# Expert input biases on two halves of the array's rows: a mixture-of-experts block on one Trainium2 core

## The chip, the cores and the metric

The kernel runs on one core of a Trainium2 chip. A core has a matrix engine (TensorE, in the profile PE, with its weight loads as PEld), a vector engine (VectorE, DVE), a scalar engine (ScalarE, ACT), a general engine (GpSimd, POOL) and a queue engine (SyncE, SP) that issues most transfers. They run side by side and wait for each other by semaphores. The metric is the device time of one execution in microseconds (us); the median over runs counts.

## The reference

The reference computes two transformer blocks on 512 tokens of 1024 numbers. The change touches the first block's mixture of experts: a router picks 4 of 32 experts for each token, and each expert, on its tokens (padded to blocks of 128), computes

```
xb = t_pad[tok_idx]                       # 128 tokens x 1024
hb = xb @ w_exp_in[e] + b_exp_in[e]       # 128 x 2048: gate columns, then value columns
g = jnp.minimum(hb[:, :D_FF], SWIGLU_LIMIT)
u = jnp.clip(hb[:, D_FF:], -SWIGLU_LIMIT, SWIGLU_LIMIT)
a = g * jax.nn.sigmoid(SWIGLU_ALPHA * g) * (u + 1.0)
return a @ w_exp_out[e] + b_exp_out[e]
```

`b_exp_in` is a table of 32 experts by 2048 columns, 1024 of the gate and 1024 of the value. It is the addition of this row that the change rearranges.

## The kernel before

All weights are float32. Each is split into a high part (a copy rounded to the matrix engine's format, by ACT, line 149, `whi`) and a low part (the difference, by DVE, line 151, `wlo`), and each product is made of three matmuls (lines 137, 138, 139: high by high, high by low, low by high). The first stage (`block1`) is a layer norm, the projections, two kinds of attention and an output projection (`out_proj`), with a layer norm and the routing tile by tile at its end. Then come the 32 experts (`moe`), one after the other, and then the second block.

An expert (`moe_h`) has four accumulators of 128 tokens x 512 columns in PSUM: `hb[0]`, `hb[1]` for the gate and `hb[2]`, `hb[3]` for the value. Each is opened with one matmul that adds the bias (line 879), and then takes 8 row blocks of `w_exp_in[e]`, three matmuls each. `swiglu` (line 884 on) makes the activation, and `moe_y` multiplies it by `w_exp_out[e]`. The second product of expert e-1 is computed while expert e is being opened, so that bias matmuls of e stand between matmuls of e-1.

The bias matmul picks a row out of the table. `self.bin` is a tile of 128 partitions x 2048 columns: rows 0 to 31 hold the high part of the 32 experts' biases, rows 32 to 63 the low part, rows 64 to 127 are zero. `self.e64` has column e equal to one in rows e and 32+e and zero elsewhere; broadcast to 128 columns it is the stationary operand, so that every token gets the row of expert e, high plus low. All 128 rows of the array are used, half of them with zeros. `moe_bias` (lines 751 to 762) loads and splits the table while the output projection of the first block runs: four transfers on POOL's queue, two ACT copies, two DVE differences, two ACT copies and a POOL memset of the zero rows.

If an expert has more than 128 tokens, `overflow` (line 963 on) handles the further blocks in a loop whose number of turns is read on the device. It has its own bias column (`ove`) on 64 rows. The inputs here make no turn of it: its tiles appear nowhere in the trace.

The order of instructions on each engine is set by a scheduler when the program is built. It also gives out the buffers: a pool `S` of 17 large buffers, a pool `H` of 10 buffers of up to 1024 numbers per partition, and four PSUM banks `mm`. A transfer into a buffer is issued when its last reader is done, and the SP queue is strictly in order. Loads of expert weights (`raw`, line 198) are issued ahead of use.

Of the kernel before, what the change touches and what calls it, by code (L numbers as in the profile page):

```python
# [11 lines left out]
F32 = mybir.dt.float32  # L12
FR = mybir.dt.float32r
# [3 lines left out]
AF = mybir.ActivationFunctionType  # L17
OP = mybir.AluOpType
AX = mybir.AxisListType
# [45 lines left out]
def f(ap):  # L65
    return ap.bitcast(F32)
# [27 lines left out]
class K:  # L94
# [539 lines left out]
    def moe_consts(self):  # L634
        nc, c, a = self.nc, self.const, self.a
        self.wr = self.slot([128, 8, 32], F32, "wr")
        nc.scalar.dma_start(self.wr, a["w_router"].rearrange("(k p) e -> p k e", p=128))
        self.br = c.tile([128, 32], F32, name="br")
        ap = a["b_router"]
        nc.scalar.dma_start(self.br, bass.AP(tensor=ap.tensor, offset=ap.offset, ap=[[0, 128], [1, 32]]))  # L640

        it = self.w([128, 512], I32, "s")
        nc.gpsimd.iota(it[:, :128], pattern=[[1, 128]], base=1, channel_multiplier=0)
        self.iota1 = c.tile([128, 128], F32, name="iota1")
        nc.vector.tensor_copy(self.iota1, it[:, :128])
        self.iota32 = c.tile([128, 32], F32, name="iota32")
        nc.vector.tensor_scalar(self.iota32, self.iota1[:, :32], -1.0, None, op0=OP.add)
        it = self.w([128, 512], I32, "s")
        nc.gpsimd.iota(it[:, :128], pattern=[[1, 128]], base=0, channel_multiplier=-1)
        self.tri = c.tile([128, 128], BF, name="tri")  # L650
        nc.vector.tensor_scalar(self.tri, it[:, :128], 0.0, None, op0=OP.is_gt)
        self.onesb = c.tile([128, 128], BF, name="onesb")
        nc.vector.memset(self.onesb, 1.0)
        self.pidx = c.tile([128, 1], F32, name="pidx")
        nc.vector.tensor_scalar(self.pidx, it[:, 0:1], -1.0, None, op0=OP.mult)
        self.pbig = c.tile([128, 1], F32, name="pbig")
        nc.vector.tensor_scalar(self.pbig, self.pidx, 4096.0, None, op0=OP.add)
        self.pidx1 = c.tile([128, 1], F32, name="pidx1")
        nc.vector.tensor_scalar(self.pidx1, self.pidx, 1.0, None, op0=OP.add)

        e64 = c.tile([128, 32], FR, name="e64")
        nc.gpsimd.memset(f(e64), 0.0)
        for i in range(2):
            sl = slice(32 * i, 32 * i + 32)
            nc.vector.tensor_copy(e64[sl, :], self.ident[sl, sl])
        self.e64 = e64
        self.selb = c.tile([128, 4, 32], BF, name="selb")
        self.posm = c.tile([128, 4, 32], F32, name="posm")

        self.V = c.tile([128, 4, 32, 6], BF, name="V")  # L670
        for i in range(4):
            nc.vector.memset(self.V[:, i, :, 1], 128.0 * i - 4096.0)
        self.m6 = c.tile([128, 6], F32, name="m6")
        nc.vector.memset(self.m6, 1.0)
        nc.vector.memset(self.m6[:, 3:4], 0.0)
        self.gate_in, self.hx = {}, {}
        self.G = c.tile([128, 4, 32], F32, name="G")
        self.ybuf = self.D.tile([2048, 1024], F32, name="ybuf")
        self.identb = c.tile([128, 128], BF, name="identb")
        nc.vector.tensor_copy(self.identb, self.ident)  # L680
# [69 lines left out]

    def moe_bias(self):
        nc, a = self.nc, self.a
        self.bin = self.slot([128, 2048], FR, "bin")
        nc.gpsimd.memset(f(self.bin[64:128, :]), 0.0)
        for c in range(2):
            sl = slice(1024 * c, 1024 * c + 1024)
            raw = self.slot([64, 1024], F32, "braw")
            for i in range(2):
                nc.gpsimd.dma_start(raw[32 * i:32 * i + 32, :], a["b_exp_in"][:, sl])
            nc.scalar.activation(self.bin[:64, sl], raw, AF.Copy)  # L760
            nc.vector.tensor_tensor(raw[32:64, :], raw[32:64, :], f(self.bin[32:64, sl]), op=OP.subtract)
            nc.scalar.activation(self.bin[32:64, sl], raw[32:64, :], AF.Copy)

    def moe_xg(self):
        xg = self.slot([128, 2, 1024], F32, "xg")
# [108 lines left out]
    def moe_h(self, xT, ones, brow, get, hb=None, beside=None):  # L874

        nc = self.nc
        hb = hb or [self.mm() for _ in range(4)]
        for n in range(4):
            nc.tensor.matmul(hb[n], ones, brow[:, n * 512:(n + 1) * 512], start=True, stop=False)
        k = n = 0  # L880
        while k < 8:
            wh, wl = get()
            for c in range(0, wh.shape[1], 512):
                at = self.mm3(hb[n], (xT[0][:, k, :], xT[1][:, k, :]), (wh[:, c:c + 512], wl[:, c:c + 512]), False, k == 7)
                k, n = k + n // 3, (n + 1) % 4
                if beside and n == 0 and k < 8:
                    with self.tc.issue_after(at.ins):
                        next(beside, 0)
        for _ in beside or ():
            pass  # L890
        return hb
# [74 lines left out]
    def overflow(self, free):  # L966

        nc, a = self.nc, self.a
        n = nc.values_load(self.nxi[0:1, 0:1], min_val=0, max_val=16)
        with self.tc.If(n > 0):  # L970
            with self.tc.For_i(0, n, 1) as j:
                t = self.slot([128, 256], F32, "ovf")
                jf, ef, bf, ecol = (t[:, x:x + 1] for x in range(4))
                cum, le, oe = t[:, 32:64], t[:, 64:96], t[:, 96:128]
# [32 lines left out]
                g = self.gates_at(oh, [V[:, i, :] for i in range(4)])  # L1007
                x = self.moe_gather(free, ix)
                xT = self.t128([x[:, :512], x[:, 512:]])
                nc.vector.tensor_scalar(ecol, self.pidx, 32.0, -32.0, op0=OP.is_ge, op1=OP.mult)  # L1010
                nc.vector.tensor_tensor(ecol, ecol, self.pidx, op=OP.add)
                e64 = self.w([64, 2], FR, "ove", 1)
                nc.vector.tensor_scalar(e64[:, 0:1], ecol[:64, :], ef[:64, :], None, op0=OP.is_equal)

                w1 = a["w_exp_in"][bass.ds(er, 1)].rearrange("o (k p) c -> p (o k) c", p=128)
                w2 = a["w_exp_out"][bass.ds(er, 1)].rearrange("o (k p) c -> p (o k) c", p=128)
# [2 lines left out]
                def get():  # L1019
# [1 line left out]
                    nc.sync.dma_start(raw, next(it))  # L1021
                    self.split(raw, hi, lo)
                    return hi, lo
                hb = self.moe_h(xT, e64[:, 0:1].to_broadcast([64, 128]), self.bin[:64, :], get)
                aT = self.t128(self.swiglu(hb), 0.5)
                self.y_out(self.moe_y(aT, get), ix, g)

# [872 lines left out]
```

## Time and profile before

| | |
|---|---|
| median of three runs | 2116.5 us (2109.83, 2116.5, 2118.72) |
| the profiled execution | 2119.69 us, its span 2117.5 us |
| busy, share of the span | PE 95%, PEld 76%, DVE 77%, ACT 60%, POOL 13% |
| mean granted TensorE clock | 0.965 of full |
| experts opened | from 444.3 to 1592.0 us |
| transfers | 513.25 MB, mean 242 GB/s |

The span is from the first to the last instruction that the profiler saw; the execution is 2.2 us longer. A matmul's row in the trace gives its start, its duration and its form. The form `128*128` is the part of the array in use, rows by columns; `64*128` is a product on 64 rows. A matmul of 512 columns lasts about 0.39 us, but the next one starts 0.23 us after it, since they are pipelined: the distance of the starts is what a matmul costs in a dense stream, not its duration. Rows that follow each other with the same line and form are merged into one, with their count.

### The profile page before, as it was taken

What the parts mean: (1) busy time and instruction counts of PE and PEld (TensorE: products, weight loads), DVE (VectorE), ACT (ScalarE), POOL (GpSimd) and SP (SyncE); (2) the same over time, 40 slices, a digit from 0 to 9 for tenths busy, and PEclk for the clock granted to TensorE, in tenths of its full rate; (3) what the DMA queues carried; (4) which work ended last, traced back from release to release, by engine and by line L of the source; (5) the groups of instructions that cost most, each with busy time, mean ns of one, the idle gap of its engine ahead of it and who ended that gap; (6) DMA issues with size and microseconds to landing.
All of it is one profiled execution on the core that took longest, in us unless ns stands there. A gap on an engine that the chain in (4) does not pass through costs nothing. (4 is left out here: it accounts for less than half of the span.)

```text
span 2117.5 us, 26074 instructions
## 1 busy us (share of the span) xinstructions
PE 2009.2 (95%) x9868; PEld 1600.5 (76%) x9868; DVE 1629.5 (77%) x2075; ACT 1272.9 (60%) x1407; POOL 274.6 (13%) x224
## 2 busy tenths in 40 slices
PE   5999999969999999999999899999999689999997
PEld 5777778847888888888888688888767578777656
DVE  5574454689898989898989789898888868557644
ACT  3554443246777777787868677786665365356540
POOL 3000000041111010101010010101115300110000
PEclk9999999979999999999999999999999799999969
DMA  5241226637999999999999899999987522242101
GB/s 192 68 147 53 70 71 210 266 120 275 348 375 362 365 367 373 356 370 359 369 359 374 308 361 355 362 370 363 375 336 276 201 73 68 67 111 69 52 32 65
DMA packets 161141, 513.25 MB, mean 242 GB/s; under 512 B 17955, under 2 KB 92995, under 8 KB 112113
## 3 DMA queue, kind: packets, MB, share of 16 engines
q1 hardware_dynamic: 139392, 466.80, 60.1%
q0 software_dynamic: 12592, 29.57, 3.9%
q10 hardware_dynamic: 9024, 15.16, 2.1%
q8 instruction: 79, 1.29, 0.2%
q14 instruction: 54, 0.43, 0.1%
HBM read 498.43 MB, written 29.49 MB: 249 GB/s over the span
## 5 line engine op out<-in xcount | busy, mean ns | idle before, releaser
L151 DVE TENSOR_TENSOR wlo<-raw,whi 128x2048 fp32r<-128x2048 f32 (+1 forms) x464 | 980.3, 2144 | 94.1 <-ACT whi L149 56.7
L149 ACT ACTIVATE whi<-raw 128x2048 fp32r<-128x2048 f32 (+1 forms) x468 | 820.8, 1785 | 161.4 <-PE sc L139 52.3
L138 PE MATMUL mm<-wlo,xT 128*128 128x512 f32 x1024 | 406.4, 397 | 1.9 <-DVE wlo L151 1.9
L139 PE MATMUL mm<-whi,xT 128*128 128x512 f32 x1024 | 404.1, 395 | 0.0
L137 PE MATMUL mm<-whi,xT 128*128 128x512 f32 x1024 | 338.0, 399 | 2.8 <-ACT whi L149 2.8
L138 PEld LDWEIGHTS mm<-wlo,xT 128*128 128x128 f32 x1024 | 194.6, 190 | 49.1 <-DVE wlo L151 11.2
L139 PEld LDWEIGHTS mm<-whi,xT 128*128 128x128 f32 x1024 | 194.2, 190 | 39.0
L137 PEld LDWEIGHTS mm<-whi,xT 128*128 128x128 f32 x1024 | 192.2, 190 | 41.4 <-ACT whi L149 3.5
L138 PE MATMUL sc<-wlo,xT 128*128 128x512 f32 x512 | 201.6, 394 | 2.1 <-DVE wlo L151 2.1
L139 PE MATMUL sc<-whi,xT 128*128 128x512 f32 x512 | 201.5, 394 | 0.0
L931 POOL DMA_INDIRECT ybuf<-h,sx x31 | 99.2, 3200 | 758.1 <-DVE wlo L151 551.6
L137 PE MATMUL sc<-whi,xT 128*128 128x512 f32 x512 | 184.9, 393 | 1.5 <-ACT xT L149 1.5
L149 ACT ACTIVATE xT<-tp 128x512 fp32r<-128x512 f32 x128 | 73.4, 595 | 161.3 <-PE tp L868 160.8
L1155 DVE CUSTOM_DVE_ANT_0 s<-sc,bias 128x512 f32<-128x512 f32 (+3 forms) x101 | 47.2, 487 | 91.8 <-PE sc L145 81.0
L138 PEld LDWEIGHTS sc<-wlo,xT 128*128 128x128 f32 x512 | 97.2, 190 | 23.6 <-DVE wlo L151 2.5
L137 PEld LDWEIGHTS sc<-whi,xT 128*128 128x128 f32 x512 | 97.4, 190 | 22.3 <-ACT xT L149 1.9
L139 PEld LDWEIGHTS sc<-whi,xT 128*128 128x128 f32 x512 | 96.9, 190 | 21.2 <-DVE xT L153 0.5
L137 PE MATMUL mm<-hTh,whi 128*128 128x512 f32 x256 | 106.6, 416 | 0.4 <-ACT whi L149 0.4
L139 PE MATMUL mm<-hTh,wlo 128*128 128x512 f32 x256 | 100.6, 393 | 0.6 <-DVE wlo L151 0.6
L138 PE MATMUL mm<-hTl,whi 128*128 128x512 f32 x256 | 100.8, 394 | 0.0
L1159 ACT ACTIVATE p<-s,mn 128x128 f32<-128x128 f32 (+3 forms) x112 | 62.2, 557 | 60.7 <-DVE mn L1155 56.4
L137 PE MATMUL mm<-xTh,whi 128*128 128x512 f32 (+1 forms) x216 | 91.5, 424 | 0.0
(451 smaller groups left out, 3105.0 us busy)
## 6 DMA issues: line engine op xcount, KB each, us to landing
raw<-in_w_exp_in_dram SPq DMA_DIRECT2D x254, 1024.0 KB, 6.9
raw<-in_w_exp_out_dram SPq DMA_DIRECT2D x128, 1024.0 KB, 7.1
raw<-in_w_in_dram SPq DMA_DIRECT2D x58, 512.0 KB, 4.2
raw<-in_w_out_dram SPq DMA_DIRECT2D x8, 1024.0 KB, 6.3
raw<-in_w_in_dram SPq DMA_DIRECT2D x7, 1024.0 KB, 7.2
yp<-ybuf POOLq DMA_DIRECT2D x12, 512.0 KB, 12.5
x<-in_x_dram SPq DMA_DIRECT2D x4, 512.0 KB, 8.3
hd<-h SPq DMA_DIRECT2D x4, 512.0 KB, 2.6
```

The costliest lines, as they stand in the source:

```text
L137: mm(out, lh, rh, start=start, stop=False, **kw)
L138: mm(out, lh, rl, start=False, stop=False, **kw)
L139: return mm(out, ll, rh, start=False, stop=stop, **kw)
L149: h = nc.scalar.activation(hi, src, AF.Copy, scale=scale)
L151: l = (eng or nc.vector).tensor_tensor(lo, src, f(hi), op=OP.subtract)
L931: self.nc.gpsimd.indirect_dma_start(out=self.ybuf[:, :], out_offset=bass.IndirectOffsetOnAxis(ap=ix[:, 1:2], axis=0), in_=y, in_offset=Non ...
L1155: nc.vector.tensor_tensor_reduce(s[:, :kl], sc[:, :kl], bias, op0=OP.add, op1=OP.min, scale=1.0, scalar=3e38, accum_out=mn)
L1159: nc.scalar.activation(p[:, :kl], s[:, :kl], AF.Exp, scale=-1.0, bias=mn, accum_out=sm)
```

## The change

The table of biases is laid out anew. Rows 0 to 31 now hold the high part of the gate's 1024 columns, rows 32 to 63 their low part, rows 64 to 95 the high part of the value's columns and rows 96 to 127 their low part. `self.bin` has 1024 columns instead of 2048, and no zero rows. `e64` has its identity in all four groups of 32 rows. A bias is added by a matmul on 64 rows: the lower half of the rows for the gate, the upper half for the value. The two follow each other in the program, gate and value of the same 512 columns, then the next 512. In the overflow loop the column `ove` gets 128 rows.

```diff
@@ moe_consts
         e64 = c.tile([128, 32], FR, name="e64")
-        nc.gpsimd.memset(f(e64), 0.0)
-        for i in range(2):
+        for i in range(4):
             sl = slice(32 * i, 32 * i + 32)
             nc.vector.tensor_copy(e64[sl, :], self.ident[sl, sl])
@@ moe_bias
-        self.bin = self.slot([128, 2048], FR, "bin")
-        nc.gpsimd.memset(f(self.bin[64:128, :]), 0.0)
-        for c in range(2):
-            sl = slice(1024 * c, 1024 * c + 1024)
-            raw = self.slot([64, 1024], F32, "braw")
-            for i in range(2):
-                nc.gpsimd.dma_start(raw[32 * i:32 * i + 32, :], a["b_exp_in"][:, sl])
-            nc.scalar.activation(self.bin[:64, sl], raw, AF.Copy)
-            nc.vector.tensor_tensor(raw[32:64, :], raw[32:64, :], f(self.bin[32:64, sl]), op=OP.subtract)
-            nc.scalar.activation(self.bin[32:64, sl], raw[32:64, :], AF.Copy)
+        self.bin = self.slot([128, 1024], FR, "bin", "S")
+        raw = self.slot([128, 1024], F32, "braw")
+        for i in range(4):
+            nc.gpsimd.dma_start(raw[32 * i:32 * i + 32, :], a["b_exp_in"][:, i // 2 * 1024:i // 2 * 1024 + 1024])
+        nc.scalar.activation(self.bin, raw, AF.Copy)
+        for i in (1, 3):
+            ps = slice(32 * i, 32 * i + 32)
+            nc.vector.tensor_tensor(raw[ps, :], raw[ps, :], f(self.bin[ps, :]), op=OP.subtract)
+            nc.scalar.activation(self.bin[ps, :], raw[ps, :], AF.Copy)
@@ moe_h
-        for n in range(4):
-            nc.tensor.matmul(hb[n], ones, brow[:, n * 512:(n + 1) * 512], start=True, stop=False)
+        for n in range(2):
+            for x, hp in enumerate((slice(0, 64), slice(64, 128))):
+                nc.tensor.matmul(hb[n + 2 * x], ones[hp, :], brow[hp, n * 512:(n + 1) * 512], start=True, stop=False)
@@ overflow
-                nc.vector.tensor_scalar(ecol, self.pidx, 32.0, -32.0, op0=OP.is_ge, op1=OP.mult)
-                nc.vector.tensor_tensor(ecol, ecol, self.pidx, op=OP.add)
-                e64 = self.w([64, 2], FR, "ove", 1)
-                nc.vector.tensor_scalar(e64[:, 0:1], ecol[:64, :], ef[:64, :], None, op0=OP.is_equal)
+                nc.vector.tensor_tensor(oe, oe, f(self.e64), op=OP.mult)
+                nc.vector.tensor_reduce(out=ecol, in_=oe, axis=AX.X, op=OP.add)
+                e64 = self.w([128, 2], FR, "ove", 1)
+                nc.vector.tensor_copy(e64[:, 0:1], ecol)
...
-                hb = self.moe_h(xT, e64[:, 0:1].to_broadcast([64, 128]), self.bin[:64, :], get)
+                hb = self.moe_h(xT, e64[:, 0:1].to_broadcast([128, 128]), self.bin, get)
```

On PE the places of the bias matmuls stay; which accumulators they open changes. These rows are of expert 3, the first that runs at the even pace of the middle of the kernel. `mm_1046` to `mm_1049` are its accumulators `hb[0]` to `hb[3]` before, `sc_1027` and `sc_1028` the output of expert 2. Before:

```order
L137 MATMUL sc_1028_4665<-whi_1021_4634,xT_994_4492 128x512
L879 MATMUL mm_1046_4758<-bin_735_3293,e64_3269 128x512
L879 MATMUL mm_1047_4759<-bin_735_3293,e64_3269 128x512
L138 MATMUL sc_1027_4664<-wlo_1022_4635,xT_994_4492 128x512
...
L137 MATMUL sc_1028_4665<-whi_1030_4668,xT_994_4492 128x512
L879 MATMUL mm_1048_4760<-bin_735_3293,e64_3269 128x512
L879 MATMUL mm_1049_4761<-bin_735_3293,e64_3269 128x512
L137 MATMUL mm_1046_4758<-whi_1033_4686,xT_1004_4544 128x512
```

The same place of the changed kernel, where `mm_1045` to `mm_1048` are `hb[0]` to `hb[3]`:

```order
L137 MATMUL sc_1027_4663<-whi_1020_4632,xT_993_4490 128x512
L879 MATMUL mm_1045_4756<-bin_735_3294,e64_3269 128x512
L879 MATMUL mm_1047_4758<-bin_735_3294,e64_3269 128x512
L138 MATMUL sc_1026_4662<-wlo_1021_4633,xT_993_4490 128x512
...
L137 MATMUL sc_1027_4663<-whi_1029_4666,xT_993_4490 128x512
L879 MATMUL mm_1046_4757<-bin_735_3294,e64_3269 128x512
L879 MATMUL mm_1048_4759<-bin_735_3294,e64_3269 128x512
L137 MATMUL mm_1045_4756<-whi_1032_4684,xT_1003_4542 128x512
```

In both, the four biases stand as two twos, twelve matmuls of the expert before apart. Before, the first two are `hb[0]` and `hb[1]`; now they are `hb[0]` and `hb[2]`, one on each half of the rows, and so for the second two. Matmuls on all 128 rows stand ahead of each two and behind it. Over the 32 experts both orders have 51 such twos (two each in experts 3 to 19 and 24 to 30, one each in 1, 2 and 31), 5 fours in a row (experts 0 and 20 to 23) and 6 single ones (two each in 1, 2 and 31).

One `H` buffer less is taken by the table, so later takers of that pool come one buffer earlier. This shows on SP's queue at the end of the first block's output projection (`raw` loads of the last quarter of `w_out`, and of the first expert's weights). Before:

```order
L228 DMA gb_742_3312<-in_ln1_b_dram 128x1024
L198 DMA raw_745_3319<-in_w_out_dram 128x4x512
L198 DMA raw_752_3433<-in_w_exp_in_dram 128x2048
L198 DMA raw_753_3435<-in_w_exp_in_dram 128x2048
L198 DMA raw_754_3437<-in_w_exp_in_dram 128x2048
L198 DMA raw_755_3439<-in_w_exp_in_dram 128x2048
L198 DMA raw_756_3441<-in_w_exp_in_dram 128x1024
L198 DMA raw_757_3443<-in_w_exp_in_dram 128x1024
```

After:

```order
L228 DMA gb_741_3310<-in_ln1_b_dram 128x1024
L198 DMA raw_755_3439<-in_w_exp_in_dram 128x1024
L198 DMA raw_756_3441<-in_w_exp_in_dram 128x1024
L198 DMA raw_744_3317<-in_w_out_dram 128x4x512
L198 DMA raw_751_3431<-in_w_exp_in_dram 128x2048
L198 DMA raw_752_3433<-in_w_exp_in_dram 128x2048
L198 DMA raw_753_3435<-in_w_exp_in_dram 128x2048
L198 DMA raw_754_3437<-in_w_exp_in_dram 128x2048
```

Two half-size loads of the first expert have moved ahead of the last quarter of `w_out`.

## Rows read from the trace of the kernel before

**Rows 1.** The page, busy time of each engine (share of the span), instructions.

```profile
PE 2009.2 (95%) x9868; PEld 1600.5 (76%) x9868; DVE 1629.5 (77%) x2075; ACT 1272.9 (60%) x1407; POOL 274.6 (13%) x224
```

**Rows 2.** Stretches: their us, busy of each engine, clock, DMA share, GB/s.

```profile
553.75:1132.12 578.37, 578.37 (x2704) 474.35 (x2702) 529.17 (x403) 440.41 (x354) 73.77 (x32) 1.00 0.96 365
589.65:625.61 35.96, 35.96 (x170) 29.57 (x169) 33.00 (x27) 27.50 (x23) 4.65 (x2) 1.00 0.97 374
```

**Rows 3.** Line 879 in 553 to 1170 and 1200 to 1510, ns min/median/max.

```profile
L879 PE MATMUL mm<-bin,e x68: 397/397/398, 553.7 to 1132.4; 128*128 128x512 f32 x68
...
L879 PE MATMUL mm<-bin,e x36: 388/397/398, 1217.9 to 1503.4; 128*128 128x512 f32 x36
```

**Rows 4.** Timeline of PE in expert 3: start, us, form, count.

```profile
553.75 0.63 PE L879 MATMUL mm<-bin,e 128*128 128x512 f32 x2
554.22 0.39 PE L138 MATMUL sc<-wlo,xT 128*128 128x512 f32 x1
...
556.97 0.63 PE L879 MATMUL mm<-bin,e 128*128 128x512 f32 x2
557.43 0.62 PE L137 MATMUL mm<-whi,xT 128*128 128x512 f32 x2
```

**Rows 5.** Timeline of PE in the attention; last, the first two of the six.

```profile
234.33 0.39 PE L139 MATMUL mm<-hTh,wlo 128*128 128x512 f32 x1
234.65 0.96 PE L145 MATMUL sc<-qk 64*128 64x512 f32 x6
235.54 0.50 PE L137 MATMUL mm<-hTh,whi 128*128 128x512 f32 x1
235.87 0.40 PE L138 MATMUL mm<-hTl,whi 128*128 128x512 f32 x1
...
234.65 0.50 PE L145 MATMUL sc<-qk 64*128 64x512 f32 x2
```

**Rows 6.** Timeline of PE in the second block, one product on 64 rows.

```profile
2004.39 0.39 PE L139 MATMUL mm<-xTh,wlo 128*128 128x512 f32 x1
2004.71 0.49 PE L145 MATMUL sc<-nk,nq 64*128 64x512 f32 x1
2005.13 0.76 PE L1178 MATMUL mm<-aT,vv 128*64 128x128 f32 x9
```

**Rows 7.** Timeline of PE in expert 22, four biases in a row.

```profile
1253.65 1.09 PE L879 MATMUL mm<-bin,e 128*128 128x512 f32 x4
1254.58 0.39 PE L137 MATMUL mm<-whi,xT 128*128 128x512 f32 x1
```

**Rows 8.** Timeline of PE in expert 2, single biases.

```profile
526.78 0.40 PE L879 MATMUL mm<-bin,e 128*128 128x512 f32 x1
...
527.49 0.40 PE L879 MATMUL mm<-bin,e 128*128 128x512 f32 x1
```

**Rows 9.** Timeline of PE, waits next to biases of experts 0, 1, 20.

```profile
449.94 0.90 PE L868 MATMUL tp<-ident,xg 128*128 128x128 f32 x3 [2.75 <-DMA xg<-h1d,sx]
...
471.66 0.50 PE L138 MATMUL sc<-wlo,xT 128*128 128x512 f32 x1 [2.06 <-DVE wlo L151]
...
1180.88 2.07 PE L879 MATMUL mm<-bin,e 128*128 128x512 f32 x4 [9.86 <-DVEq L970]
```

**Rows 10.** Timeline of PE in expert 31.

```profile
1578.70 1.20 PE L879 MATMUL mm<-bin,e 128*128 128x512 f32 x2
1580.10 2.07 PE L798 MATMUL sc<-bout,gT 32*128 32x512 f32 x2 [0.20 <-DVE acc L800]
```

**Rows 11.** Timeline of SP and ACT at the first output projection.

```profile
367.90 0.38 SPq L198 DMA_DIRECT2D raw<-in_w_out_dram  x1
371.98 23.45 SPq L198 DMA_DIRECT2D raw<-in_w_exp_in_dram  x11
...
390.83 1.92 ACT L149 ACTIVATE whi<-raw 128x2048 fp32r<-128x2048 f32 x1 [14.31 <-DMA raw<-in_w_exp_in_dram]
```

**Rows 12.** SP waits in 553 to 1130: us in total, times, longest.

```profile
SPq L198 <- PE sc L139: 187.3, 65, 3.5
```

## Prediction

> **What bounds the kernel now.** I read the page first: PE is busy 95% of the span, far ahead of the next engine, DVE at 77% [rows 1]. A share over the whole kernel is a mean over stages, so the second view is a table of stretches. From 553.75 to 1132.12 us, experts 3 to 19, PE is busy for all 578.37 us, at full granted clock; DVE is busy 529.17 of them, ACT 440.41, and the DMA engines 96% [rows 2]. One expert is 35.96 us, with PE busy for all of it [rows 2]. A PE that is full by the trace may still wait inside matmuls whose ends are modelled, so I looked at the queue that feeds it: SP's weight loads wait for PE to free a buffer (187.3 us in 65 waits for one line alone) [rows 12]. The transfers are held back by PE and not the other way round. What PE gains or loses per expert goes straight into the time.
>
> The third view is line 879, the bias matmuls. In experts 3 to 19 there are 68 of them, in experts 21 to 29 another 36, all of them on 128 by 128 of the array [rows 3]. What one costs is read from distances of starts: the first two of expert 3 hold the engine from 553.75 to 554.22, the second two from 556.97 to 557.43 [rows 4], so 0.465 us for two and 0.93 us for an expert, of 35.96.
>
> **The price of a product on 64 rows.** Does a two on halves of the rows cost one slot instead of two? The kernel has such products already, in the attention (line 145, form 64\*128). Of six of them, all of 512 columns, the first two together end 0.50 us after the start of the first, while one lasts 0.49 [rows 5, 6]: they run side by side, and a two is one slot of 0.23 us.
>
> But the six also show what it costs to get there and back. From the start of the last full product ahead of them, 234.33, to the start of the second full product behind, 235.87, there are 1.54 us [rows 5]. In these lie five slots: a full product, three twos, a full product, 5 x 0.23 = 1.15. The other 0.39 us are the price of leaving the full array and coming back. Where it lies: the first two start 0.32 after the full product (0.09 late), the full product behind them is followed by the next only after 0.33 (0.10 late), and 0.20 are between [rows 5]. A single product of 512 columns shows the middle: 0.32 from the full product to it, and 0.42 from it to the next one in another form [rows 6], which with 0.33 at the end gives 0.09 + 0.19 + 0.10 = 0.38, the same sum.
> The Trainium skill, "TensorEngine Tiling (Array Packing)", Key Properties, says that going to another tiling mode drains TensorE. The trace agrees, with 0.39 us for the way there and back.
>
> **The sum.** A two before is 0.465; after it is 0.23 + 0.39 = 0.62, so 0.155 us more. The order leaves the places as they were, two twos per expert with full products between them.
> - Experts 3 to 19 and 24 to 30 have 48 twos, and experts 1 and 2 one each: 50 x 0.155 = 7.75 us.
> - Experts 21 to 23 have their four in a row, 0.93 us [rows 7]; after it is two slots and one way there and back, 0.46 + 0.39 = 0.85. 3 x -0.08 = -0.2.
> - Expert 20 opens at the lower clock, its four taking 2.07 us [rows 9]. Two of four slots go, two costlier changes come: -0.3, between -0.8 and +0.1.
> - Expert 2 has two single biases [rows 8]. A product on 64 rows takes a full slot, and each pays both ways: 2 x 0.39 = +0.8.
> - Expert 1's two single ones stand ahead of waits of PE, 2.75 us for gathered tokens and 2.06 us for a DVE difference [rows 9], which take up 0.4 each; the first wait covers expert 0's four as well. Cost 0.
> - Expert 31's stand among products of forms that are not full anyway (32\*128) [rows 10], so the changes of form are paid today: -0.1.
>
> Together 7.75 - 0.2 - 0.3 + 0.8 - 0.1 = 7.95, say 8 us.
>
> The trace shows no single two of 512 columns between full products, so I bound the 0.39. From below: if only the middle part is paid, 0.19 [rows 6], a two costs 0.42 and 50 of them save 2.3 us; with two singles at 0.19 and the other places -1, the whole is -3. From above: 0.19 at either end and 0.10 at the last, 0.48, gives 50 x 0.245 = 12.3 and 13 in all. I take 0.39, the row with the same form, length and neighbours.
>
> Beside the bias matmuls, the table is made differently while the output projection runs. ACT has three copies instead of four, DVE the same two differences, POOL loses a memset and keeps four transfers. ACT's first copy now waits for all four transfers, so that the DVE difference behind it, and the split of `w_out` behind that, can come about 1 us later; PE takes that split a few matmuls later in the new order. 0 to +1 us, taken as 0. On SP's queue two expert loads of 512 KB now stand ahead of the last quarter of `w_out`. That quarter was issued at 367.90, and the first expert load at 371.98 [rows 11]. If all is held until then, 2 MB at the 365 GB/s of [rows 2] take 6 us, until 378; ACT took it at 390.83 [rows 11]. 12 us are to spare, and the expert's own loads come early. Cost 0; without that cover it would be 4 us. The overflow loop is not entered. The memset of `e64` that goes and two small copies that come lie at the very start, where PE waits for other things: 0.
>
> Against the profiled execution, 2119.7 + 8 = 2127.7. It lies 3.2 us above the median, so for the median 2116.5 + 8 = **2124.5**, 0.38% more.
>
> **Rivals.**
> *The halves run side by side and the change of form is free.* Then a two saves 0.235, 50 of them 11.8 us, and the fours of experts 20 to 23 about 2: 2103. For it: the starts of the twos [rows 5]. Against it: 0.39 us in the same rows, and 0.38 in others. 6%.
> The Trainium skill, "TensorE: Matmul & The Clock Gate", Part 3 (Packing small matmuls), gives this rival as a rule: the span of products packed into one array is that of one, plus about 4 ns for each further tile. The rows bear it out inside a run of such products and not at its ends.
>
> *PE's longer expert is taken up elsewhere.* DMA engines are 96% busy [rows 2]; if their pace set the expert's length, PE could grow for nothing, and the time would be 2116.5 to 2118. Against it: SP waits for PE, and PE has no gap. 8%.
>
> *The two halves do not overlap here,* say because one weight load holds up the other. Then a two takes 0.46 + 0.39 = 0.85 and the 50 cost 19 us: 2136, clearly slower. For it: here every product brings its own weights, and each half of the six did too. Against it: 0.50 us for two. 5%.
>
> *The first output projection stalls* by the later table or by the `w_out` quarter: 4 us on top of the 8, 2128.5. It decides if that quarter lands after 390.83. 5%.
>
> **How the numbers follow.** The forecast has 76%; its own range, from the spread of the runs shown (2110 to 2119) and the smaller errors of the sum, is 2119 to 2131. About 0.5%, 10.6 us, is what a measurement of this kernel can tell from no change: up to 2127.1 is no change. The forecast lies 2.6 us below that line, so of its 76% about 24 are beyond it; with the last two rivals, 5 and 2, slower has 31%. Faster is the first rival, 6%. The rest is 63%. The range that leaves out the free change of form and the top of the serial case is 2113 to 2135.
>
> **What would show it.** In the changed profile line 879 has form 64\*128, its twos merged to 0.50 us instead of 0.63. If I am right, the next full product starts 0.42 after the first of a two, the one behind it 0.33 later, the product ahead 0.32 before; expert 3 to expert 4 is 36.27 us instead of 35.96; PE stays full from 554 to 1140. Fours take 0.66 to the next start instead of 0.93, and 0.10 more behind it. If the next expert still comes after 35.96, the second rival is right; after 35.5, the first; after 36.75, the third. The prediction is wrong if the expert's length does not grow, or if the time moves by 8 us while it does not.

## The result and the profile after

| | before | after |
|---|---|---|
| median of 8 runs each | 2111.36 us (2109.14 to 2118.72) | 2126.0 us (2120.6 to 2132.5) |
| profiled execution | 2119.69 us | 2126.33 us, its span 2124.2 us |
| mean granted clock | 0.965 | 0.964 |

The ratio is 1.0068, with a 95% interval of 1.005 to 1.0086: the changed kernel is 14.6 us slower (10.6 to 18). The forecast was 8 us more. That the median lies only 1.5 us above the forecast 2124.5 is partly luck: with eight runs the kernel before came out at 2111.4, not at the 2116.5 of the first three. The profiled execution of before is slower than all eight of these, so the two traces are only 6.6 us apart at the end; where the time goes is read from the stages, not from the ends.

The page of the profile after (busy time, share of the span, instructions) answers to [rows 1]:

```profile
PE 2020.6 (95%) x9868; PEld 1586.3 (75%) x9868; DVE 1628.2 (77%) x2077; ACT 1271.5 (60%) x1406; POOL 260.1 (12%) x222
```

PE is still what bounds the kernel, and it is busy 11.4 us longer. Stretches of the changed kernel (length, busy time of each engine, clock, DMA share, GB/s), experts 3 to 19 and one expert, against [rows 2]:

```profile
558.70:1139.35 580.65, 580.65 (x2691) 463.02 (x2690) 525.99 (x400) 438.41 (x353) 68.28 (x32) 1.00 0.96 361
594.91:631.21 36.30, 36.30 (x171) 29.03 (x170) 33.01 (x26) 27.49 (x23) 4.32 (x2) 1.00 0.99 381
```

PE is busy for all of both, at full clock, with DMA at 0.96 as before. Line 879 in experts 3 to 19 and 21 to 29 (ns min/median/max, first and last start, form), against [rows 3]:

```profile
L879 PE MATMUL mm<-bin,e x68: 497/497/497, 558.7 to 1142.7; 64*128 64x512 f32 x68
...
L879 PE MATMUL mm<-bin,e x36: 385/497/497, 1227.3 to 1514.3; 64*128 64x512 f32 x36
```

The form is now 64\*128 and nothing stands on 128\*128 any more. From the first bias of expert 3 to the last of expert 19 it is 1142.7 - 558.7 = 584.0 us; less the 3.4 us between the first and the last bias of one expert, that is 580.6 for 16 experts, 36.29 us each. By [rows 3] it was 1132.4 - 553.7 less 3.45 ([rows 4]), 35.95 us. The timeline of PE in expert 3 of the changed kernel (start, us, form, count) shows why:

```profile
558.15 0.61 PE L137 MATMUL sc<-whi,xT 128*128 128x512 f32 x2
558.70 0.50 PE L879 MATMUL mm<-bin,e 64*128 64x512 f32 x2
559.13 0.50 PE L138 MATMUL sc<-wlo,xT 128*128 128x512 f32 x1
559.47 0.39 PE L139 MATMUL sc<-whi,xT 128*128 128x512 f32 x1
```

The two biases count 0.50 us together instead of 0.63. But the next full product starts 0.43 after them, the one behind it 0.34 later, and the second of the two products ahead (it starts 0.23 after 558.15) starts 0.32 ahead of them, where a dense stream has 0.23 each time. Four in a row, in expert 22, against [rows 7]:

```profile
1262.69 0.39 PE L139 MATMUL sc<-whi,xT 128*128 128x512 f32 x1
1263.01 0.73 PE L879 MATMUL mm<-bin,e 64*128 64x512 f32 x4
1263.66 0.50 PE L137 MATMUL mm<-whi,xT 128*128 128x512 f32 x1
1264.00 0.40 PE L138 MATMUL mm<-wlo,xT 128*128 128x512 f32 x1
```

Here it is 0.65 us to the next start instead of 0.93, and 0.34 from that to the one behind it.

The second place where the kernel lost time is the first output projection. Waits of PE in 365 to 400 us of the changed kernel (us in total, times, longest):

```profile
PE mm L138 <- DVE wlo L151: 1.8, 1, 1.8
```

The kernel before has no wait there. The matmul that waits needs the low part of the second quarter of `w_out`. Before, DVE ended it 0.16 us ahead of PE's need: PE's matmul starts at 375.42, the split ends at 372.97 + 2.29 = 375.26. Timeline of before: ACT's two copies of the table, DVE's split, PE's matmul, SP's loads.

```profile
365.85 1.06 ACT L760 ACTIVATE bin<-braw 64x1024 fp32r<-64x1024 f32 x1 [0.85 <-DMA braw<-in_b_exp_in_dram]
367.43 1.06 ACT L760 ACTIVATE bin<-braw 64x1024 fp32r<-64x1024 f32 x1 [0.52 <-DMA braw<-in_b_exp_in_dram]
...
372.97 2.29 DVE L151 TENSOR_TENSOR wlo<-raw,whi 128x2048 fp32r<-128x2048 f32 x1
...
375.42 0.39 PE L138 MATMUL mm<-wlo,mTh 128*128 128x512 f32 x1
...
342.64 0.37 SPq L198 DMA_DIRECT2D raw<-in_w_out_dram  x1
355.02 0.34 SPq L228 DMA_DIRECT2D gb<-in_ln_g_dram  x1
356.29 0.34 SPq L228 DMA_DIRECT2D gb<-in_ln_b_dram  x1
```

After, the same lines:

```profile
370.25 1.06 ACT L757 ACTIVATE bin<-braw 128x1024 fp32r<-128x1024 f32 x1 [4.87 <-DMA braw<-in_b_exp_in_dram]
...
371.35 1.22 DVE L760 TENSOR_TENSOR braw<-braw,bin 32x1024 f32<-32x1024 f32 x1 [3.04 <-ACT bin L757]
...
376.37 2.29 DVE L151 TENSOR_TENSOR wlo<-raw,whi 128x2048 fp32r<-128x2048 f32 x1
...
378.71 0.50 PE L138 MATMUL mm<-wlo,mTh 128*128 128x512 f32 x1 [1.84 <-DVE wlo L151]
...
355.38 0.37 SPq L198 DMA_DIRECT2D raw<-in_w_out_dram  x1
358.12 0.34 SPq L228 DMA_DIRECT2D gb<-in_ln_g_dram  x1
360.65 0.34 SPq L228 DMA_DIRECT2D gb<-in_ln_b_dram  x1
```

ACT's one copy of the table starts at 370.25, when the last of its four transfers has landed; DVE's difference waits 3.04 us for it, and the split behind that difference in DVE's order starts 3.4 us later than before. PE waits 1.84 us. And on SP the third quarter of `w_out` was issued at 355.38 instead of 342.64, with the two loads of layer norm weights (`gb`) behind it, at 358.12 and 360.65 instead of 355.02 and 356.29. SP's waits in 335 to 375, first of before, then of after:

```profile
SPq L228 <- DMA ybuf<-z: 12.9, 2, 12.0
...
SPq L198 <- DMA raw<-in_w_branch_b_dram: 2.3, 1, 2.3
```

```profile
SPq L198 <- DMA ybuf<-z: 14.3, 1, 14.3
```

In the changed program this load has to wait for a semaphore that ACT's zeroing transfers to `ybuf` signal; before, it waited for the load of `w_branch_b`, 2.3 us, and it was the load of `gb` behind it that waited for the zeroing transfers, 12.0 us. ACT's own loads have moved too: the loads of residual rows (`hr`, 512 KB each), of which before three, after all four have been issued by 372 us:

```profile
360.58 0.33 ACTq L1801 DMA_DIRECT2D hr<-hd  x1
...
362.62 0.33 ACTq L1801 DMA_DIRECT2D hr<-hd  x1
...
371.78 0.33 ACTq L1801 DMA_DIRECT2D hr<-hd  x1
```

```profile
358.77 2.82 ACTq L1801 DMA_DIRECT2D hr<-hd  x3
...
362.95 0.33 ACTq L1801 DMA_DIRECT2D hr<-hd  x1
```

So more is under way on the DMA engines while the table is loaded. The stretch from 355 to 371 us (length, busy times, clock, DMA share, GB/s), first of before, then of after:

```profile
355.00:371.00 16.00, 16.00 (x72) 13.25 (x71) 11.22 (x14) 7.68 (x8) 3.80 (x5) 1.00 0.99 282
```

```profile
355.00:371.00 16.00, 16.00 (x72) 13.27 (x71) 8.14 (x10) 3.81 (x4) 2.00 (x4) 1.00 1.03 334
```

How far the stages have slipped is read by taking the same place in PE's order in two traces and subtracting the starts. Each number is the start in that trace less the start in the first trace of before, in us, at five places (the time in before is given), with the run's measured difference beside it (the runs are explained below):

| run | expert 0 (444) | expert 3 (554) | expert 19 (1132) | expert 31's product ended (1642) | end | measured |
|---|---|---|---|---|---|---|
| after | 4.1 | 5.0 | 10.5 | 12.2 | 6.6 | +14.6 |
| after, again | 2.0 | 2.8 | 8.0 | 10.0 | 10.6 | +13.5 |
| before, again | -0.7 | -1.4 | -1.4 | -2.5 | -5.8 | +0.3 |
| full products, new table | 3.9 | 3.4 | 3.2 | 1.2 | 1.7 | +3.4 |
| halves, two raw tiles | -1.0 | 0.2 | 5.4 | 5.5 | 2.1 | +11.4 |
| 64 rows, one by one | 0.2 | 1.8 | 14.9 | 23.8 | 14.2 | +27.5 |
| changed kernel, copy cut in two | 0.2 | 0.9 | 6.4 | 9.5 | 5.6 | +10.8 |
| changed kernel, second buffer | -0.6 | -0.7 | 4.3 | 3.9 | 7.6 | +7.4 |

From expert 3 to 19 the five traces with half-row biases side by side agree: they slip 5.0 to 5.6 us, and the kernel before against itself not at all (-0.1). From expert 0 to 1642 the changed kernel slips by 8.1 us in both of its traces; that these two are so close is chance, since the other three slip 6.5, 9.3 and 4.5 us, and the kernel before against itself -1.7. Behind 1642 the traces differ by several us with no order that follows the change, two traces of the kernel before among them (3.3 us).

### The profile page after: what moved, and what is told of

Same layout as the page of the kernel before. It is cut to its first block, busy times and chain, and to the rows that moved or that the text cites. A ratio compares the mean times of both kernels' runs of the same rounds, so it can differ in the third digit from the quotient of the medians.

```text
span 2124.2 us, 26069 instructions
## 1 busy us (share of the span) xinstructions
PE 2020.6 (95%) x9868; PEld 1586.3 (75%) x9868; DVE 1628.2 (77%) x2077; ACT 1271.5 (60%) x1406; POOL 260.1 (12%) x222
## 5 line engine op out<-in xcount | busy, mean ns | idle before, releaser
L138 PEld LDWEIGHTS mm<-wlo,xT 128*128 128x128 f32 x1024 | 194.4, 190 | 48.2 <-DVE wlo L151 10.6
L931 POOL DMA_INDIRECT ybuf<-h,sx x31 | 91.4, 2949 | 767.9 <-ACT h L927 705.9
```

The lines of the kernel that those rows point to most:

```text
L138: mm(out, lh, rl, start=False, stop=False, **kw)
L931: self.nc.gpsimd.indirect_dma_start(out=self.ybuf[:, :], out_offset=bass.IndirectOffsetOnAxis(ap=ix[:, 1:2], axis=0), in_=y, in_offset=Non ...
```

## The experiments

**The front end alone.** The new table and the new order of the biases, with full products: two one-hot columns per expert instead of one.

```diff
-            for x, hp in enumerate((slice(0, 64), slice(64, 128))):
-                nc.tensor.matmul(hb[n + 2 * x], ones[hp, :], brow[hp, n * 512:(n + 1) * 512], start=True, stop=False)
+            for x in range(2):
+                nc.tensor.matmul(hb[n + 2 * x], ones[x], brow[:, n * 512:(n + 1) * 512], start=True, stop=False)
```

> The new table (1024 columns on 128 rows, one raw tile) with its own preparation and the new order of the biases, but every bias is added by a matmul on all 128 rows; two one-hot columns per expert pick the gate's or the value's half, the other half meets zeros. So the way in which the table is made is as in the changed kernel, and no product leaves the full array. Theory (two causes: form changes about +8 us, a stall of the first output projection about +3): +3 us against the kernel before (2 to 4), expert 3 to 4 is 35.96 us, the bias rows read 128*128 again, and PE still waits about 1.8 us for the low part of w_out near 377 us. Rival A (all of it is the form changes): 0 against before. Rival B (all of it is the preparation of the table): +10 to +14.

Measured: ratio 1.0016 (1.0004 to 1.0029), +3.4 us. Line 880 here is the bias, and PE's wait:

```profile
L880 PE MATMUL mm<-bin,e x68: 388/397/398, 557.1 to 1135.6; 128*128 128x512 f32 x68
...
PE mm L138 <- DVE wlo L151: 2.5, 1, 2.5
```

(1135.6 - 557.1 - 3.5) / 16 = 35.94 us per expert: no growth without the halves, and the wait is there without them. Rivals A and B are out.

**The halves alone.** Half-row biases, and the table in two steps, each with a raw tile (the buffer it is loaded into) of its own, as in the kernel before.

```diff
-        raw = self.slot([128, 1024], F32, "braw")
...
+        for c in range(2):
+            raw = self.slot([128, 1024], F32, "braw")
+            hp, lp = slice(64 * c, 64 * c + 64), slice(64 * c + 32, 64 * c + 64)
...
+            nc.scalar.activation(self.bin[hp, :], raw[hp, :], AF.Copy)
```

> The changed kernel with its half-row bias products, but the table is split in two steps as before: gate and value each through a raw tile of its own, so that the order on ACT, SP and POOL's transfers is that of the kernel before. Theory: the stall of the first output projection is gone and the form changes stay: +8 us against before (7.5 to 9), expert 3 to 4 is 36.29 us. Rival A: +11 to +14 still. Rival B: 0.

Measured: 1.0054 (1.0037 to 1.0071), +11.4 us (7.8 to 15). No wait of PE near 377, and the halves as they were:

```profile
L879 PE MATMUL mm<-bin,e x68: 497/497/498, 553.9 to 1137.6; 64*128 64x512 f32 x68
```

(1137.6 - 553.9 - 3.4) / 16 = 36.27 us. The expert is as expected, the stall is gone, but the whole is 3 us above the 8 expected, which lie just inside the interval; its trace up to 1642 shows 6.5 more than at expert 0. With the front end alone, +3.4, the two parts add up to 14.8, about the whole.

**Halves without side by side.** The kernel before, each bias on rows 0 to 63.

```diff
-            nc.tensor.matmul(hb[n], ones, brow[:, n * 512:(n + 1) * 512], start=True, stop=False)
+            nc.tensor.matmul(hb[n], ones[:64, :], brow[:64, n * 512:(n + 1) * 512], start=True, stop=False)
```

> The kernel before with its table; each bias matmul uses only rows 0 to 63 of the array (the rows that hold anything), one after the other. It pays the changes of form and has nothing side by side. Theory: a two costs 0.465 + 0.39 = 0.855 us instead of 0.465; 50 twos are 19.5 us, with fours and single ones about +21 us against before, expert 3 to 4 is 36.74 us. Rival A, form changes dearer than 0.39 (0.5 to 0.6): +26 to +31, 36.95 to 37.15 us. Rival B, form changes free: 0.

Measured: 1.013 (1.0106 to 1.0154), +27.5 us (22 to 33); in the trace +23.6 from expert 0 to 1642.

```profile
554.98 0.61 PE L137 MATMUL sc<-whi,xT 128*128 128x512 f32 x2
555.52 0.72 PE L879 MATMUL mm<-bin,e 64*128 64x512 f32 x2
556.18 0.50 PE L138 MATMUL sc<-wlo,xT 128*128 128x512 f32 x1
556.51 0.40 PE L139 MATMUL sc<-whi,xT 128*128 128x512 f32 x1
...
L879 PE MATMUL mm<-bin,e x68: 385/441/497, 555.5 to 1147.5; 64*128 64x512 f32 x68
```

The next full product now comes 0.66 after the first of a two, 0.23 later than with both halves at once; (1147.5 - 555.5 - 4.0) / 16 = 36.75 us per expert, expected 36.74. So in the changed kernel the halves do run side by side, and the change of form costs 0.39 to 0.40. All but the size of the total (21 expected) is as the theory said.

**Four in a row, two ways.** First, halves and two raw tiles, biases held until the output product beside them has ended (`behind` places instructions after a given one):

```diff
+        with self.behind(self.last_y):
+          for n in range(2):
+            for x, hp in enumerate((slice(0, 64), slice(64, 128))):
+                nc.tensor.matmul(hb[n + 2 * x], ones[hp, :], brow[hp, n * 512:(n + 1) * 512], start=True, stop=False)
...
-                self.mm3(yb[n], (aT[0][:, k, :], aT[1][:, k, :]), (wh[:, c:c + 512], wl[:, c:c + 512]), k == 0, k == 7)
+                self.last_y = self.mm3(yb[n], (aT[0][:, k, :], aT[1][:, k, :]), (wh[:, c:c + 512], wl[:, c:c + 512]), k == 0, k == 7)
```

> As the run with two raw tiles (the table's preparation as before), and the four half-row biases of an expert held back until the output product beside them has ended, so that they stand in a row in experts 3 to 30 and pay one way to the other form and back. Theory: four cost 0.46 + 0.39 = 0.85 us instead of 0.93 before: -0.08 per expert, about -2.5 us against before (0 to -4), expert 3 to 4 is 35.88 us. Rival A (the price is paid per product, not per run of products): +8 or more, 36.3 us. Rival C: the later biases let PE wait where DVE or ACT were hidden before: a wait in front of the first products of each expert, +0.1 us or more per expert, +3 us and more.

Measured: 0.9985 (0.9973 to 0.9997), -3.2 us. Line 880 is the bias:

```profile
L880 PE MATMUL mm<-bin,e x68: 384/441/497, 559.9 to 1130.7; 64*128 64x512 f32 x68
```

(1130.7 - 559.9 - 0.3) / 16 = 35.66 us: 0.22 less than expected, so something else had changed too. Its order showed what: held back that far, the biases let the transposes and the first products of the next expert fall into other places. Two runs take this apart. The kernel before with the same hold on its full products:

```diff
+        with self.behind(self.last_y):
+          for n in range(4):
+            nc.tensor.matmul(hb[n], ones, brow[:, n * 512:(n + 1) * 512], start=True, stop=False)
```

> The kernel before with its full-array biases, held back until the output product beside them has ended: four in a row, in the same order of instructions as the run 'fours' on PE, ACT and SP; only the form of the bias products differs from that run. It tells what of fours' gain (35.655 us per expert instead of 35.95, where 35.88 was expected) comes from the halves. Theory: a four costs 0.93 instead of 0.85, so 0.08 more than in 'fours': 35.73 us per expert, and against before -0.22 x 28 = -6 us up to the end of the experts from the other places of transposes and products. Rival (the gain is from the halves alone): 35.95 us and 0.

Measured: 0.9972 (0.9956 to 0.9989), -6 us, the fastest of all. And halves that are moved back by twelve matmuls only, with all else in place (`self.first` is the first of three matmuls of a product):

```diff
+        with self.behind(self.y_late):
...
+                if (k, n) == (6, 1):
+                    self.y_late = self.first
```

> Half-row biases with the table prepared in two steps as before (no stall), the first two of an expert moved back by twelve matmuls to stand with the second two; nothing else moves, so that transposes and products stand as in the kernel before. One way to the half-row form and back per expert instead of two. Theory: expert 3 to 4 is 36.28 - 0.39 - 0.02 = 35.87 us, 0.08 below the kernel before; against before -1.5 us (-3 to 0) up to the end of the experts. Rival A (price per product): 36.28 us, +7. Rival B (grouping gains what 'fours' gained): 35.65 us, -8.

Measured: 0.9991 (0.9977 to 1.0005), -1.9 us, not told from zero. The biases of both, first the full ones in the far place, then the halves in the near one:

```profile
L880 PE MATMUL mm<-bin,e x68: 388/396/398, 558.1 to 1130.2; 128*128 128x512 f32 x68
```

```profile
L880 PE MATMUL mm<-bin,e x68: 384/441/497, 556.6 to 1130.2; 64*128 64x512 f32 x68
```

They give (1130.2 - 558.1 - 0.7) / 16 = 35.71 and (1130.2 - 556.6 - 0.3) / 16 = 35.83 us. One trip to the halves and back per expert instead of two is worth 36.27 - 35.83 = 0.44, where 0.41 was expected; the price is per trip and not per product. The far place is worth 35.95 - 35.71 = 0.24 with full products and 35.83 - 35.66 = 0.17 with the halves; the halves save 0.05 in it and 35.95 - 35.83 = 0.12 in the near one, where 0.08 was expected for both. What in the far place saves the time was not tried.

**What the comparison itself shows, and the change once more.** Both programs as they are, without an edit.

> The kernel before, once more, against itself: what a comparison shows where nothing differs, and a second trace of it. In the first trace 17.1 us lie between the first product of yt with ohT (1658.1) and the first transpose of h behind it (1675.2); in the traces of the changed kernel and of three experiments it is 11.0 to 11.6. Theory (that was chance in one profiled execution, which was also 7 us above the median): ratio 1.000 within 0.0015, and 11 to 12 us in that stretch. Rival (something in the kernel before makes that stretch longer): 17 us again.

Measured: 1.0001 (0.9985 to 1.0018). The stretch named is 11.7 us long in this trace (1656.0 to 1667.7), and 18.2 in that of a later run with half-row biases: its length is chance of one execution. The comparison itself adds nothing.

> The changed kernel once more, on the same chip as these controls. Theory: the form changes (+8 us up to the end of the experts) and the stall at the first output projection (+4) add up to +12 us, 1.0057, with the run that keeps full products (+3.4 measured) and the run with two raw tiles (+11.4 measured, of which +6 to +7 is in its trace up to the end of the experts) as parts. Rival (parts that no trace shows): +15 us or more. In the trace: PE waits about 1.8 us for wlo near 377 us again, expert 3 to 4 is 36.30 us again.

Measured: 1.0064 (1.0037 to 1.0091), +13.5 us. PE waits again; the same stretch in both traces of the changed kernel (length, busy times, clock, DMA share, GB/s), first the first:

```profile
376.00:384.00 8.00, 6.16 (x20) 4.63 (x19) 6.07 (x5) 2.77 (x3) 0.00 (x0) 0.79 1.04 414
```

```profile
376.00:384.00 8.00, 5.85 (x27) 4.77 (x27) 6.89 (x6) 2.24 (x2) 0.00 (x0) 1.00 1.04 420
...
PE mm L138 <- DVE wlo L151: 2.1, 1, 2.1
```

In the first trace the clock fell behind the wait, to 0.79 over these 8 us (0.50, the lower of its two levels, from 380 to 382), and the place cost 3.7 us (the slip goes from 0.4 to 4.1); in the second it did not fall, and the place cost 2.4 (-0.5 to 1.9). +12 was expected; the interval holds 12 and 15.

**What makes PE wait.** Two things had changed: the late load of `w_out`, which with the loads bunched beside and behind it crowds the table's transfers, and one copy that waits for four transfers. One run keeps the late load and cuts the copy in two:

```diff
-        nc.scalar.activation(self.bin, raw, AF.Copy)
+        for c in range(2):
+            hp = slice(64 * c, 64 * c + 64)
+            nc.scalar.activation(self.bin[hp, :], raw[hp, :], AF.Copy)
```

> The changed kernel (one raw tile of 128 rows, half-row biases), with ACT's copy of the table cut in two copies of 64 rows, so that the first waits for its own two transfers only. The order on SP stays that of the changed kernel, and the third quarter of w_out is still issued late (near 355 us instead of 342, behind the zeroing transfers of ybuf). Theory L (the stall near 377 us comes from the transfers that bunch up behind that late load, so that the table lands near 370 us instead of 366 to 367): PE still waits 1 to 2 us for wlo, +11 to +14 against before. Theory W (it comes from one copy that waits for all four transfers): the wait of PE is gone or under 0.3 us, the sum is +8 to +9.

Measured: 1.0051 (1.003 to 1.0072), +10.8 us. ACT's copies, the table's landings seen by them, and PE's wait:

```profile
366.22 1.06 ACT L759 ACTIVATE bin<-braw 64x1024 fp32r<-64x1024 f32 x1 [1.56 <-DMA braw<-in_b_exp_in_dram]
369.28 1.06 ACT L759 ACTIVATE bin<-braw 64x1024 fp32r<-64x1024 f32 x1 [1.99 <-DMA braw<-in_b_exp_in_dram]
...
PE mm L138 <- DVE wlo L151: 0.2, 1, 0.2
```

The other keeps the one copy and takes a small second buffer, which puts SP's order back, and with it the loads of `hr`:

```diff
+        raw2 = self.slot([128, 8], F32, "braw")
+        nc.gpsimd.memset(raw2, 0.0)
```

> The reverse: one raw tile and one ACT copy that waits for all four transfers, as in the changed kernel, but a small second buffer (8 columns, set to zero, read by nobody) is taken from the pool beside it, which puts the order on SP back to that of the kernel before; the third quarter of w_out is then issued at about 342 us. Half-row biases stay. Theory L: the table lands at 367 to 368 us, PE waits under 0.7 us for wlo near 376 us, and the sum is +8 to +10 against before. Theory W: PE waits about 1.8 us as in the changed kernel, +11 to +14.

Measured: 1.0035 (1.0018 to 1.0051), +7.4 us. The table is complete at 364.97, and PE has no wait:

```profile
364.97 1.06 ACT L759 ACTIVATE bin<-braw 128x1024 fp32r<-128x1024 f32 x1 [2.46 <-DMA braw<-in_b_exp_in_dram]
```

Neither theory was right alone. With the late load the second pair of transfers lands near 369.3 instead of 367.4, and the first at 366.2; two copies live with that (0.23 us of wait), one copy does not, since DVE's first difference, and with it all behind it on DVE, then waits for the second pair. One copy with early transfers costs nothing either. The stall of 2 us takes both. Two things are not separated. Which of the crowding loads holds the table up, that of `w_out`, of `gb` or of `hr`, is open, since the last run moves all of them. And its table is complete 2.5 us earlier than the second pair landed in the kernel before (367.43): by an estimate from that trace, one copy started then would end at 368.49, 0.5 us behind the start of DVE's first difference there (367.95), with 0.16 to spare, so a small stall from the one copy alone is not excluded.

## Why the prediction was right and where it was wrong

- *The price of a two (0.155 us).* Right. The expert grew by 36.29 - 35.95 = 0.34 us, 0.17 for each of its two twos, and the starts are those named ahead: 0.43, 0.34 and 0.32 where 0.42, 0.33 and 0.32 stood. The 0.39 us for leaving the full array and coming back, read from [rows 5], measured 0.39 to 0.40 with the halves one by one.
- *Fours, singles, the ends.* Right in sum: from expert 0 to 1642 the changed kernel slipped 8.1 us in both traces, forecast 7.95, though so close a match is luck (4.5 to 9.3 in the other three traces with the same biases). Read matmul by matmul, the pieces fit as well. Expert 2's two singles take 2.41 us (530.42 to 532.83) instead of 1.64 (526.32 to 527.96), 0.77 more, forecast 0.8. Expert 20's four with what stands ahead of the next line 139 takes 2.49 us (1190.10 to 1192.59) instead of 3.05 (1180.88 to 1183.93), 0.56 less, forecast 0.3. The branch ahead of expert 20 moves by 1 us between two traces of the same kernel, so sums over it are no better than that.
- *The change of form is free; the longer expert is taken up elsewhere; the halves do not overlap.* All three are out, by 36.29 us per expert (35.5, 35.95 and 36.75 would have been theirs), the last also by the run that has no overlap and does show 36.75.
- *The table's preparation: "0 to +1 us, taken as 0", and the rival with a stall of the first output projection.* This is the step that failed. It cost 2.4 and 3.7 us in the traces of the changed kernel and 4.4 in that of the run with full products, which measured 3.4 as a whole. The rival had the place, and at 4 us the price, but got 5% and hung on the last quarter of `w_out`, for which there was cover. I had looked at the queue where its order changes, and not at the third quarter, whose place in SP's order is the same and whose wait is another. And I had not read how much PE could spare for the second quarter: 0.16 us. With that row, "1 us later" could not have been put at 0.
- *The whole.* 8 forecast, 14.6 (10.6 to 18) and 13.5 (7.8 to 19) measured. The two traces show 8.1 and 2.4 to 3.7, 10.5 to 12 together. The other 2 to 3 us are within the intervals; if they are real, they lie behind the experts, where two traces of one kernel differ by as much, and that stays open. The two runs with the same biases and no stall measured 11.4 and 7.4, on either side of the 8. The absolute time came out near the forecast since the base had been taken 5 us too high.

The Trainium skill, "TensorE: Matmul & The Clock Gate", Part 3 (Packing small matmuls), says that PE pulls a weight load ahead of running matmuls where it goes to row groups that do not conflict, or to the background weight buffer. In the dense stream here, where every load and every matmul has all 128 rows, the loads do run ahead; across the change of form the trace shows none that does. Weight loads of the changed kernel (start, us, form, count, idle time before) beside the starts in expert 3 shown above:

```profile
558.70 0.18 PEld L879 LDWEIGHTS mm<-bin,e 64*128 64x128 f32 x2 [0.35 <-issue]
559.13 0.19 PEld L138 LDWEIGHTS sc<-wlo,xT 128*128 128x128 f32 x1 [0.24 <-issue]
559.24 0.19 PEld L139 LDWEIGHTS sc<-whi,xT 128*128 128x128 f32 x1
```

The loads for the halves begin at 558.70 with their own matmuls, and so does the load for the full product behind, at 559.13; the next one, at 559.24, is again 0.23 ahead of its matmul at 559.47. On the way out and on the way back, the weight load starts with its matmul and not ahead of it.

## What to carry to other kernels

Products on part of the array save a slot and cost a trip: here 0.39 us for the way there and back, against 0.23 for a slot of 512 columns, so that a lone two loses and only a row of four or more between full products gains. Put such products together, or leave them on the full array. And when a change touches how data are prepared, read how long the consumer could wait for each piece, and look at the waits of transfers whose place in the queue has not changed too: which semaphore they wait for may have.

## What was not expected

Holding all biases of an expert back behind the output product made the kernel before 0.24 us per expert faster (35.71 instead of 35.95) with no half-row product at all, 0.9972 of its time; of all versions tried it is the fastest, 2107.0 us. The 0.05 us per expert that the halves save on top (35.66) cannot be told by the timing (0.9985 of before, and the intervals overlap). A wait of PE of 1.84 us was followed by a fall of the granted clock to its lower level in one execution (0.79 as the mean of 8 us), one of 2.1 us in another execution of the same program by none (1.00), and one of 2.5 us in the run with full products again by a fall (0.79).

One name in the text ahead is to be mended: the output product that stands beside expert 3's biases is that of expert 1, by its weights, not of expert 2: there it is the product of expert e-2, and not of e-1, that runs while expert e is opened. No number rests on it.
